# Edits at five places of an encoder layer on one core: first row, product order, bias table, rotation tables, a joint

## The chip, the core and the metric

One core of a Trainium2 chip runs the whole layer in one launch. The metric is the device time of the execution in microseconds; the median of three runs counts. TensorE (PE) multiplies, VectorE (DVE), ScalarE (ACT) and GpSimd (POOL) do the rest, and SyncE (SP), ACT and POOL issue DMAs.

## What is computed

A layer on x of 512 tokens by 1024 features, in float32: a feed-forward half step, a mixer of two attentions, a second feed-forward half step, and a last norm.

```python
def swiglu(x, w1, w3, w2):
    return (jax.nn.silu(x @ w1) * (x @ w3)) @ w2

x = x + 0.5 * swiglu(rmsnorm(x, ffn1_norm), w1, w3, w2)      # d_ff = 2816
x = x + hybrid_mixer(rmsnorm(x, mix_norm), ...)              # A and B below
x = x + 0.5 * swiglu(rmsnorm(x, ffn2_norm), w1, w3, w2)
return rmsnorm(x, final_norm)
# A: 3 groups x 8 heads, dilated windows; scores get bias_tab[t5_bucket(rel_steps * dilation)]
# B: 8 query heads on 2 key heads; q and k are RMS-normed, scaled by a gain, and rotated:
#    [x0 * cos - x1 * sin, x0 * sin + x1 * cos]
```

The bias of A depends only on the head and on the distance, so it is a table of 32 buckets by 24 heads, spread over 383, 255 and 255 distances for the three groups.

## The kernel before

**Numbers.** Every float32 product is made of three products of a shorter kind (fp32r). An operand X is split into a high part (a cast: wh, hH, TH) and a low part (X minus the high part: wl, hL, TL). `mm3` (L260) issues high by high, high by low and low by high: L262, L263 and L264 in every row. ACT does the casts (L247 for weights), DVE the low parts (L248).

**Layout and order.** x lies feature by token: eight rows x[d] of 128 features by 512 tokens. The order of PE is the order of the program (`manual_schedule`); the other engines' queues are ordered by the planner, by priority and by when it thinks an input ready. A tile is a buffer of a ring with a tag; a new tile in a full ring waits until all that read or wrote an earlier one has ended. Weights run through rings of three (wr raw, wh and wl split), loaded by SP and split some chunks ahead of PE.

**The start** (`layer`, from L1257). After four warm-up products (`idle`, L266), for each row d: SP loads x[d] and, for d < 4, the part of the first weights that multiplies it; `norm_h` (L406) makes hH on ACT, then hL on DVE (the norm's own factor comes in later, from the running squares); the weight part is cast on ACT (L1274) and its low part made on DVE (L1275). For d = 0 the weight part comes as two quarters of 256 columns, all on SP's queue behind x[0]. `quad` (L287) makes the first four features at once: for each row k, for each of four banks c, one mm3. It, and all features by `feat` (L277), use four main banks of PSUM (tag mm); four side banks (tag aux) serve the rest. What comes out of the first four features is held back until the norm's factor R is there (`stat_R`, a hook at step 33); feature 4 (f = 2) goes to a side bank meanwhile.

**The bias table.** After the first Strassen group, `blocks` multiplies by w2: eight output rows d, and at the end of row d = 0, 1 and 2 (`side`) `bias_rows(d)` is called (L683): SP loads the one-hot table and the mask into one tile of tag c1 (two buffers, shared with the Strassen accumulators); one PE product by `self.rel` (L692); DVE adds the mask in place (L693); POOL's queue stores the row from the tile to DRAM (L694). Rows 0 and 1 are interleaved (`sequence`, lag 2): row 0 ends, then two blocks of row 1, then row 1 ends. Later `bias_spread` copies the rows for the heads.

**The rotation tables** (`rope_tables`, L1043) are gain times cosine or sine, made on DVE in four token blocks, two halves, two functions and two gains, when PE is in the gate features; these are evicted by DVE as z (L730).

**The joint.** In `mixer`, w_out gives x its last addition row by row; `done_o(d)` (L1248) adds, makes hH and hL of the row, then, for d >= 4, `t_rows` (L867) combines rows d-4 and d into operands of the second feed-forward's Strassen steps (TH and TL, L884 and L885, and the upper half of hH, hL). PE goes on with steps A11, A12 (bank X, all rows of hH and hL), A11 of the next pair, S1 (bank Y, TH and TL).

Of the kernel before, what the change touches and what calls it, by code (L numbers as in the profile page):

```python
# [11 lines left out]
F32 = mybir.dt.float32  # L12
# [21 lines left out]
LAST = 2  # L34
WARM = 4
T = 512
# [34 lines left out]
class Layer:  # L71
    def __init__(self, ctx, tc, a):
# [20 lines left out]
        nc.vector.memset(self.eps, EPS)  # L93
        nc.scalar.activation(self.ones, self.ones, AF.Copy)
        self.r = c.tile([128, 8], F32, name="r")
# [191 lines left out]
    def quad(self, name, done):  # L287
        banks = [self.bank() for _ in range(4)]
        for k in range(NK):
            if k % 2 == 0:  # L290
                H, L = self.weights(name, k // 2)
            for c in range(4):
                s = slice(512 * (k % 2) + 128 * c, 512 * (k % 2) + 128 * c + 128)
                self.mm3(banks[c], H[:, s], L[:, s], self.hH[k], self.hL[k], k == 0, k == NK - 1)
                if k == NK - 1:
                    done[c](banks[c])
                yield

# [106 lines left out]

    def norm_h(self, d, g, n=T):  # L406
        nc = self.nc
        gc = self.par[:, g + d:g + d + 1]
        H, L, x = self.hH[d][:, :n], self.hL[d][:, :n], self.x[d][:, :n]
        self.lead = nc.scalar.activation(H, x, AF.Copy, scale=gc)  # L410
        nc.vector.scalar_tensor_tensor(L, x, gc, f32(H), op0=ALU.mult, op1=ALU.subtract)  # L411

# [69 lines left out]
    def ffn_run(self, s, gin, gnext, hooks, out=None, side={}):  # L482
# [193 lines left out]
    def bias_open(self, bp):  # L676
        self.bp = bp
        self.rel = bp.tile([32, 64], F32, name="rel_bias")[:, :24]
        self.nc.sync.dma_start(self.rel, self.a["rel_bias"])
        self.zd = self.dram.tile([8, 128, NV], F32, name="zd")  # L680
        self.vd = self.dram.tile([8, NV], F32, name="vd")

    def bias_rows(self, g):  # L683
        nc = self.nc
        n = (V0, V1, V2)[g]
        o = (0, V0, V0 + V1)[g]
        both = self.cp.tile([128, 1024], F32, tag="c1", name="bias")
        t = {"onehot": both[:32, :n], "vmask": both[:8, 512:512 + n]}
        for k in t:
            nc.sync.dma_start(t[k], self.a[k][:, o:o + n])  # L690
        ps = self.aux("bps")
        nc.tensor.matmul(ps[:8, :n], self.rel[:, 8 * g:8 * g + 8], t["onehot"], start=True, stop=True)  # L692
        nc.vector.scalar_tensor_tensor(t["vmask"], ps[:8, :n], 8.0, t["vmask"], op0=ALU.mult, op1=ALU.add)  # L693
        nc.gpsimd.dma_start(self.vd[:, o:o + n], t["vmask"])  # L694

# [171 lines left out]
    def t_rows(self, d):  # L867
# [14 lines left out]
        for src, H, L in ((raw[:, 0:3], self.TH[:, k], self.TL[:, k]),  # L882
                          (raw[:, 3], self.hH[k][:, 256:512], self.hL[k][:, 256:512])):
            nc.scalar.copy(H, src)  # L884
            nc.vector.tensor_sub(L, src, f32(H))  # L885

# [156 lines left out]
    def rope_tables(self, bp):  # L1043
# [6 lines left out]
        for w in range(2):  # L1050
            GC = bp.tile([128, 4, 2, 64], F32, name=f"GC{w}")
            GS = bp.tile([128, 4, 2, 64], F32, name=f"GS{w}")
            for i in range(4):
                for half in range(2):
                    for dst, e in ((GC, 0), (GS, 1)):
                        nc.vector.scalar_tensor_tensor(dst[:, i, half], gq[:, w, half], 1.0 if w else HD_B ** -0.5, cs[:, i, e],
                                                       op0=ALU.mult, op1=ALU.mult)
            self.tabs.append((GC, GS))
# [103 lines left out]
    def mixer(self):  # L1162
# [149 lines left out]
def constants():  # L1312
# [4 lines left out]
    ok = np.concatenate([np.abs(d0) <= 64, np.abs(d1) <= 64, d2 % 4 == 0])  # L1317
    onehot = (np.arange(N_BUCKETS)[:, None] == t5_bucket(rel)[None, :]).astype(np.float32)
    vmask = np.broadcast_to(np.where(ok, 0.0, 8.0 * NEG).astype(np.float32), (8, NV))
    t = np.arange(T)  # L1320
# [79 lines left out]
```

## Time and profile before

| | us |
|---|---|
| median of three runs | 1244.58 (1244.53 to 1245.4) |
| the profiled execution | 1244.16 |
| its span | 1242.4 |
| PE busy | 1233.9 |
| DVE busy | 906.8 |
| ACT busy | 605.8 |
| POOL busy | 126.5 |

The span runs from the first instruction to the last; the time has 1.8 us around it. Busy times overlap. A product's recorded duration reaches into the next one, so the pitch (start to start) tells what it costs PE; PEld is the weight load beside it. In a time line a bracket shows how long the engine was idle before a row and what ended that.

### The profile page before, as it was taken

The numbers are of one execution on the slowest core, as the hardware profiler recorded it, in microseconds if no ns is written. First come the engines' busy times: TensorE is split into PE (matmuls) and PEld (weight loads), VectorE is DVE, ScalarE is ACT, GpSimd is POOL, SyncE is SP. The second block draws the span as 40 slices with busy tenths as digits, with TensorE's granted clock in tenths as the row PEclk, the third lists the DMA queues.
The fourth block names the chain that finished last, engine by engine and source line by source line (L and its number), as shares of the span: only waits on it lengthen the run. The fifth ranks groups of instructions, "written<-read, shape, count | busy, mean of one in ns | idle before, by whom it ended". The sixth has DMA issues, their size and how long they took to land.

```text
span 1242.4 us, 20511 instructions
## 1 busy us (share of the span) xinstructions
PE 1233.9 (99%) x8228; PEld 1116.0 (90%) x8228; DVE 906.8 (73%) x1371; ACT 605.8 (49%) x897; POOL 126.5 (10%) x131
## 2 busy tenths in 40 slices
PE   9999999999999999999999999999999999999998
PEld 7897999899899999988888888888899989988997
DVE  6985688468787887567746888865988757875874
ACT  7652365245464444454424446664665425532554
POOL 1111101000222110200001200000211001100001
PEclk9999999999999999999999999999999999999999
DMA  8785777241388982662232231267768536744222
GB/s 292 220 217 166 194 195 194 92 119 52 136 222 251 231 229 97 223 183 79 87 116 100 68 119 43 71 218 241 208 170 203 157 99 188 189 149 111 60 85 68
DMA packets 90224, 190.85 MB, mean 154 GB/s; under 512 B 12801, under 2 KB 18577, under 8 KB 90129
## 3 DMA queue, kind: packets, MB, share of 16 engines
q1 hardware_dynamic: 70912, 145.46, 34.5%
q0 software_dynamic: 18496, 43.54, 17.6%
q8 instruction: 64, 1.05, 0.4%
q10 hardware_dynamic: 720, 0.55, 0.1%
q14 instruction: 32, 0.25, 0.1%
HBM read 175.79 MB, written 17.38 MB: 155 GB/s over the span
## 4 chain that ended last, share of the span: by engine, by line
PE 92%; DVE 3%; DMA 2%; issue 1%; ACT 0%; SPq 0%; POOL 0%; POOLq 0%; ACTq 0%; DVEq 0%
PE mm L262 23%; PE mm L264 22%; PE mm L263 22%; PE Y L263 4%; PE Y L262 4%; PE Y L264 4%; PE X L263 2%; PE X L264 2%; PE X L262 2%; DMA wt<-in_w13b 1%; PE S L925 1%; PE mm L1001 1%; PE Tb L1137 1%; PE T L1012 1%; DVE wl L248 1%
## 5 line engine op out<-in xcount | busy, mean ns | idle before, releaser
L247 ACT CAST wh<-wr 128x1024 fp32r<-128x1024 f32 x133 | 139.6, 1050 | 182.2 <-PE mm L263 124.1
L248 DVE TENSOR_TENSOR wl<-wr,wh 128x1024 fp32r<-128x1024 f32 x133 | 163.0, 1225 | 52.1 <-ACT wh L247 51.5
L262 PE MATMUL mm<-hH,wh 128*128 128x256 f32 (+1 forms) x560 | 179.7, 321 | 0.4 <-DVE t L509 0.3
L264 PE MATMUL mm<-hH,wl 128*128 128x256 f32 (+1 forms) x560 | 177.0, 316 | 0.0
L263 PE MATMUL mm<-hL,wh 128*128 128x256 f32 (+1 forms) x560 | 176.9, 316 | 0.0
L262 PE MATMUL mm<-gg,wh 128*128 128x512 f32 (+1 forms) x440 | 166.4, 378 | 0.0
L263 PE MATMUL mm<-gg,wh 128*128 128x512 f32 (+1 forms) x440 | 165.9, 377 | 0.0
L264 PE MATMUL mm<-gg,wl 128*128 128x512 f32 (+1 forms) x440 | 165.9, 377 | 0.0
L262 PEld LDWEIGHTS mm<-hH,wh 128*128 128x128 f32 x560 | 105.2, 188 | 9.9 <-ACT wh L1274 1.1
L264 PEld LDWEIGHTS mm<-hH,wl 128*128 128x128 f32 x560 | 105.2, 188 | 8.4 <-DVE wl L1275 0.4
L263 PEld LDWEIGHTS mm<-hL,wh 128*128 128x128 f32 x560 | 105.3, 188 | 7.4 <-DVE hL L411 0.2
L247 ACT CAST wh<-wa 128x1024 fp32r<-128x1024 f32 x54 | 56.8, 1051 | 96.3 <-PE mm L263 46.1
L262 PEld LDWEIGHTS mm<-gg,wh 128*128 128x128 f32 x440 | 82.6, 188 | 16.6 <-PE mm L264 0.9
L264 PEld LDWEIGHTS mm<-gg,wl 128*128 128x128 f32 x440 | 82.6, 188 | 15.3
L263 PEld LDWEIGHTS mm<-gg,wh 128*128 128x128 f32 x440 | 82.6, 188 | 15.0
L247 ACT CAST wh<-ws 128x1024 fp32r<-128x1024 f32 x54 | 56.8, 1052 | 71.3 <-PE mm L263 49.3
L247 ACT CAST wh<-wt 128x1024 fp32r<-128x1024 f32 x54 | 56.8, 1052 | 64.9 <-PE mm L263 41.4
L262 PE MATMUL mm<-TH,wh 128*128 128x256 f32 x320 | 88.4, 276 | 0.0
L263 PE MATMUL mm<-TL,wh 128*128 128x256 f32 x320 | 88.3, 276 | 0.0
L264 PE MATMUL mm<-TH,wl 128*128 128x256 f32 x320 | 88.3, 276 | 0.0
L248 DVE TENSOR_TENSOR wl<-wt,wh 128x1024 fp32r<-128x1024 f32 x54 | 65.9, 1222 | 28.7 <-ACT wh L247 27.9
L581 DVE TENSOR_TENSOR u<-mm,R 128x512 f32<-128x512 f32 x40 | 27.7, 691 | 75.7 <-PE mm L264 75.5
(280 smaller groups left out, 3240.6 us busy)
## 6 DMA issues: line engine op xcount, KB each, us to landing
wr<-in_w2a SPq DMA_DIRECT2D x22, 512.0 KB, 3.3
wt<-in_w13b SPq DMA_DIRECT2D x22, 512.0 KB, 3.5
wa<-in_w13b SPq DMA_DIRECT2D x22, 512.0 KB, 3.3
wt<-in_w13b POOLq DMA_DIRECT2D x22, 512.0 KB, 6.0
wr<-in_w2b SPq DMA_DIRECT2D x22, 512.0 KB, 3.7
wt<-in_w13a SPq DMA_DIRECT2D x18, 512.0 KB, 3.8
wt<-in_w13a POOLq DMA_DIRECT2D x18, 512.0 KB, 7.1
wa<-in_w13a SPq DMA_DIRECT2D x18, 512.0 KB, 3.9
```

Of the source, the lines that this page charges most:

```text
L247: self.nc.scalar.copy(H, raw)
L248: self.nc.vector.tensor_sub(L, raw, f32(H))
L262: mm(out, lH, rH, start=start, stop=False, skip_group_check=more)
L263: mm(out, lH, rL, start=False, stop=False, skip_group_check=more)
L264: mm(out, lL, rH, start=False, stop=stop, skip_group_check=more)
L581: nc.vector.tensor_mul(u, ps, R)
L925: nc.tensor.matmul(*args, start=True, stop=True)
L1001: nc.tensor.matmul(oc, v, p, start=st, stop=sp)
L1012: nc.tensor.transpose(ps[:, 128 * b:128 * b + 128], P[h][:, c0 + 128 * b:c0 + 128 * b + 128], self.ident)
L1137: nc.tensor.transpose(pt[:, 128 * j:128 * j + 128], P[h, j][:, 128 * k:128 * k + 128], self.ident)
```

## The change

At the start, x row 0's weight quarters are loaded from ACT's queue, ahead of the row loop, and the dummy activation on `ones` moves behind them; a warm-up product goes. `norm_h` for row 0 makes only hH, one half of the columns on ACT and one on DVE; DVE casts the first weight quarter; then comes hL (`low`), and low parts of weights are queued behind hL. `quad` issues, for all rows but the last, first the four high by high products, then the four with hL, then the four with wl. Feature 5 goes to a side bank as feature 4 does. The bias table becomes an fp32r product over 64 rows: the table's high part over its low part, and the one-hot table twice, cast on ACT into a tile of its own (counts made even by zero columns). The rotation tables are made for four token blocks in one operation. At the joint, one low part of TL (k = 2, made in `t_rows(6)`) is put off until behind row 7's hL.

```diff
-WARM = 4
+WARM = 3
-        nc.scalar.activation(self.ones, self.ones, AF.Copy)      # in __init__
 quad:
+            terms = [(w, h, c) for w, h in ((H, self.hH[k]), (H, self.hL[k]), (L, self.hH[k])) for c in range(4)]
+            for n, (w, h, c) in enumerate(terms):
+                self.nc.tensor.matmul(banks[c], w[:, s[c]], h, start=k == 0 and n < 4, stop=False)
+                if n % 3 == 2:
+                    yield
 norm_h:
+        if first:
+            nc.scalar.activation(H[:, :256], x[:, :256], AF.Copy, scale=gc)
+            nc.vector.tensor_scalar(H[:, 256:], x[:, 256:], gc, None, op0=ALU.mult)
+            return
 plain:
-                yield from self.feat("w13" + s, 2 * f + 1, later(done3))
+                yield from self.feat("w13" + s, 2 * f + 1, later(done3), f == 2)
 bias_open:
+        raw = bp.tile([64, 32], F32, name="rel_bias")[:, :24]
+        self.rel = bp.tile([64, 32], F32R, name="relr")[:, :24]
+        for e in range(2):
+            nc.sync.dma_start(raw[32 * e:32 * e + 32], self.a["rel_bias"])
+        with self.tc.issue_after(self.lead.ins):
+            nc.scalar.copy(self.rel, raw)
+        with self.tc.issue_after(self.lowest.ins):
+            nc.vector.tensor_sub(self.rel[32:64], raw[32:64], f32(self.rel)[32:64])
 bias_rows:
         both = self.cp.tile([128, 1024], F32, tag="c1", name="bias")
-        t = {"onehot": both[:32, :n], "vmask": both[:8, 512:512 + n]}
+        m, vmask = (n + 1) // 2 * 2, both[:8, 512:512 + n]
+        nc.sync.dma_start(both[:64, :m], self.a["onehot"][:, o + g:o + g + m])
+        nc.sync.dma_start(vmask, self.a["vmask"][:, o:o + n])
+        onehot = self.cp.tile([128, 1024], F32R, tag="c1", name="onehot")[:64, :m]
+        nc.scalar.copy(onehot, both[:64, :m])
-        nc.tensor.matmul(ps[:8, :n], self.rel[:, 8 * g:8 * g + 8], t["onehot"], start=True, stop=True)
+        nc.tensor.matmul(ps[:8, :m], self.rel[:, 8 * g:8 * g + 8], onehot, start=True, stop=True)
 t_rows:
+            if k == 2 and src.shape[1] == 3:
+                self.owed = (L, src, f32(H))
 rope_tables:
-            for i in range(4):
-                for half in range(2):
+            for half in range(2):
+                g = gq[:, w, half].unsqueeze(1).to_broadcast([128, 4, 64])
+                for dst, e in ((GC, 0), (GS, 1)):
+                    nc.vector.scalar_tensor_tensor(dst[:, :, half], g, 1.0 if w else HD_B ** -0.5, cs[:, :, e],
+                                                   op0=ALU.mult, op1=ALU.mult)
 done_o:
+            if d == 7:
+                with tc.issue_after(self.lowest.ins):
+                    nc.vector.tensor_sub(*self.owed)
 layer:
+        for s in (slice(0, 256), slice(256, 512)):
+            nc.scalar.dma_start(self.raws[0][:, s], self.a["w13a"][0][:, s])
+        nc.scalar.activation(self.ones, self.ones, AF.Copy)
-            for s in parts:
+            for s in parts[:len(parts) * d]:
                 nc.sync.dma_start(self.raws[d // 2][:, s], self.a["w13a"][d // 2][:, s])
-            self.norm_h(d, G_FFN1)
+            self.norm_h(d, G_FFN1, first=d == 0)
-                nc.scalar.copy(H[:, s], raw[:, s])
-                nc.vector.tensor_sub(L[:, s], raw[:, s], f32(H)[:, s])
+                (nc.scalar.copy if d or s.start else nc.vector.tensor_copy)(H[:, s], raw[:, s])
+                if d == 0 and s.start == 0:
+                    self.low(d, G_FFN1, T)
+                with tc.issue_after(self.lowest.ins):
+                    nc.vector.tensor_sub(L[:, s], raw[:, s], f32(H)[:, s])
```

## Rows read from the trace of the kernel before

**Rows 1.** The page, busy times and instructions of each engine.
```profile
PE 1233.9 (99%) x8228; PEld 1116.0 (90%) x8228; DVE 906.8 (73%) x1371; ACT 605.8 (49%) x897; POOL 126.5 (10%) x131
```

**Rows 2.** Time line, start: start, us, engine, line, operation, out<-in, count [idle before <-releaser].
```profile
1.32 3.78 PE L269 MATMUL warm<-R 128*128 128x256 f32 x8 [1.32 <-POOL R L97]
3.90 0.72 ACT L410 ACTIVATE hH<-x,par 128x512 fp32r<-128x512 f32 x1 [1.22 <-DMA par<-in_par]
4.96 0.80 PE L262 MATMUL mm<-hH,wh 128*128 128x512 f32 x1
5.28 0.40 ACT L1274 CAST wh<-wr 128x256 fp32r<-128x256 f32 x1 [0.36 <-DMA wr<-in_w13a]
5.56 0.61 PE L263 MATMUL mm<-hL,wh 128*128 128x512 f32 x1
6.01 0.40 PE L264 MATMUL mm<-hH,wl 128*128 128x512 f32 x1
6.24 0.40 PE L262 MATMUL mm<-hH,wh 128*128 128x512 f32 x1
6.60 0.72 ACT L410 ACTIVATE hH<-x,par 128x512 fp32r<-128x512 f32 x1 [0.92 <-DMA x<-in_x]
...
11.69 0.39 PE L262 MATMUL mm<-hH,wh 128*128 128x512 f32 x1
```

**Rows 3.** Time line, a DVE operation of 256 columns.
```profile
905.15 0.42 DVE L877 SCALAR_TENSOR_TENSOR Traw<-Traw 128x256 f32<-128x256 f32 x1
```

**Rows 4.** Windows: stretch; busy PE, PEld, DVE, ACT, POOL; clock, DMA share, GB/s.
```profile
2.00:4.00 2.00, 2.00 (x6) 1.59 (x5) 0.00 (x0) 0.77 (x3) 0.00 (x0) 1.00 0.85 245
4.00:5.00 1.00, 1.00 (x4) 0.38 (x2) 0.35 (x1) 0.91 (x2) 0.00 (x0) 1.00 0.67 156
```

**Rows 5.** Time line, PE at 35 us.
```profile
34.59 0.39 PE L264 MATMUL mm<-hH,wl 128*128 128x512 f32 x1
35.25 0.50 PE L262 MATMUL mm<-hH,wh 128*128 128x512 f32 x1 [0.27 <-DVE t L509]
```

**Rows 6.** The chain that ended last: start, us, what; the bias products.
```profile
99.62 0.73 PE bps L692 x2
...
101.94 0.52 PE bps L692 x2
...
108.15 0.52 PE bps L692 x2
```

**Rows 7.** Waits of SP's queue, 82 to 112 us: total, times, longest.
```profile
SPq L690 <- DMA vd<-bias: 5.0, 1, 5.0
```

**Rows 8.** Time line, the first store and the third load of the bias table.
```profile
101.23 0.58 POOL L694 DMA_DIRECT2D vd<-bias  x1 [17.58 <-DVE bias L693]
...
103.06 0.31 SPq L690 DMA_DIRECT2D bias<-in_onehot  x1
```

**Rows 9.** Line L1056's cosine operations (as many sine ones); time line, PE behind them.
```profile
L1056 DVE SCALAR_TENSOR_TENSOR GC<-gq,cs x16: 217/218/226, 638.9 to 643.0; 128x64 f32<-128x64 f32 x16
...
643.31 0.39 PE L264 MATMUL mm<-wh,hL 128*128 128x512 f32 x1
644.00 0.50 PE L262 MATMUL mm<-wh,hH 128*128 128x512 f32 x1 [0.30 <-DVE z L730]
```

**Rows 10.** Time line, the joint.
```profile
902.68 0.95 DVE L885 TENSOR_TENSOR TL<-Traw,TH 128x768 fp32r<-128x768 f32 x1
...
903.55 0.74 DVE L411 SCALAR_TENSOR_TENSOR hL<-x,par,hH 128x512 fp32r<-128x512 f32 x1
...
904.35 0.38 PE L263 MATMUL X<-hL,wh 128*128 128x256 f32 x1 [0.26 <-DVE hL L411]
...
909.03 0.95 DVE L885 TENSOR_TENSOR TL<-Traw,TH 128x768 fp32r<-128x768 f32 x1
```

**Rows 11.** Windows, the joint, columns as above.
```profile
904.30:907.90 3.60, 3.55 (x31) 3.56 (x32) 3.60 (x8) 3.02 (x5) 1.10 (x1) 1.00 0.34 120
```

**Rows 12.** Windows, the end of the span.
```profile
1238.00:1239.00 1.00, 0.00 (x0) 0.00 (x0) 0.26 (x1) 0.00 (x0) 0.26 (x1) 0.57 0.94 307
```

More of the change, by code (lines that the diff above doesn't have):

```diff
@@ L291, in quad @@
                 H, L = self.weights(name, k // 2)
[L292 to L295, printed above, removed]
-                    done[c](banks[c])
-                yield
+            last = k == NK - 1
+            s = [slice(512 * (k % 2) + 128 * c, 512 * (k % 2) + 128 * c + 128) for c in range(4)]
+            if last:
+                for c in range(4):
+                    self.mm3(banks[c], H[:, s[c]], L[:, s[c]], self.hH[k], self.hL[k], False, True)
+                    done[c](banks[c])
+                    yield
+                continue
+            terms = [(w, h, c) for w, h in ((H, self.hH[k]), (H, self.hL[k]), (L, self.hH[k])) for c in range(4)]
+            for n, (w, h, c) in enumerate(terms):
+                self.nc.tensor.matmul(banks[c], w[:, s[c]], h, start=k == 0 and n < 4, stop=False)
+                if n % 3 == 2:
+                    yield
     def token(self, name, n, toks, done):
@@ L404, in weave, with norm_h, low @@
                 next(fill, None)
-    def norm_h(self, d, g, n=T):
+    def norm_h(self, d, g, n=T, first=False):
         nc = self.nc
         gc = self.par[:, g + d:g + d + 1]
+        H, x = self.hH[d][:, :n], self.x[d][:, :n]
+        if first:
+            nc.scalar.activation(H[:, :256], x[:, :256], AF.Copy, scale=gc)
+            nc.vector.tensor_scalar(H[:, 256:], x[:, 256:], gc, None, op0=ALU.mult)
+            return
+        self.lead = nc.scalar.activation(H, x, AF.Copy, scale=gc)
+        self.low(d, g, n)
+    def low(self, d, g, n):
         H, L, x = self.hH[d][:, :n], self.hL[d][:, :n], self.x[d][:, :n]
-        self.lead = nc.scalar.activation(H, x, AF.Copy, scale=gc)
-        nc.vector.scalar_tensor_tensor(L, x, gc, f32(H), op0=ALU.mult, op1=ALU.subtract)
+        self.lowest = self.nc.vector.scalar_tensor_tensor(L, x, self.par[:, g + d:g + d + 1], f32(H), op0=ALU.mult, op1=ALU.subtract)
     def norm_sq(self, d, pool=NK - 2):
@@ L677, in bias_open @@
         self.bp = bp
-        self.rel = bp.tile([32, 64], F32, name="rel_bias")[:, :24]
-        self.nc.sync.dma_start(self.rel, self.a["rel_bias"])
+        nc = self.nc
+        raw = bp.tile([64, 32], F32, name="rel_bias")[:, :24]
[6 more added lines that the diff above has]
+            nc.vector.tensor_sub(self.rel[32:64], raw[32:64], f32(self.rel)[32:64])
         self.zd = self.dram.tile([8, 128, NV], F32, name="zd")
@@ L687, in bias_rows @@
         both = self.cp.tile([128, 1024], F32, tag="c1", name="bias")
-        t = {"onehot": both[:32, :n], "vmask": both[:8, 512:512 + n]}
-        for k in t:
-            nc.sync.dma_start(t[k], self.a[k][:, o:o + n])
+        m, vmask = (n + 1) // 2 * 2, both[:8, 512:512 + n]
[3 more added lines that the diff above has]
+        nc.scalar.copy(onehot, both[:64, :m])
         ps = self.aux("bps")
-        nc.tensor.matmul(ps[:8, :n], self.rel[:, 8 * g:8 * g + 8], t["onehot"], start=True, stop=True)
-        nc.vector.scalar_tensor_tensor(t["vmask"], ps[:8, :n], 8.0, t["vmask"], op0=ALU.mult, op1=ALU.add)
-        nc.gpsimd.dma_start(self.vd[:, o:o + n], t["vmask"])
+        nc.tensor.matmul(ps[:8, :m], self.rel[:, 8 * g:8 * g + 8], onehot, start=True, stop=True)
+        nc.vector.scalar_tensor_tensor(vmask, ps[:8, :n], 8.0, vmask, op0=ALU.mult, op1=ALU.add)
+        nc.gpsimd.dma_start(self.vd[:, o:o + n], vmask)
     def bias_spread(self, h):
@@ L884, in t_rows @@
             nc.scalar.copy(H, src)
-            nc.vector.tensor_sub(L, src, f32(H))
+            if k == 2 and src.shape[1] == 3:
+                self.owed = (L, src, f32(H))
+            else:
+                nc.vector.tensor_sub(L, src, f32(H))
     def until(self, fill, item):
@@ L1052, in rope_tables @@
             GS = bp.tile([128, 4, 2, 64], F32, name=f"GS{w}")
-            for i in range(4):
-                for half in range(2):
-                    for dst, e in ((GC, 0), (GS, 1)):
-                        nc.vector.scalar_tensor_tensor(dst[:, i, half], gq[:, w, half], 1.0 if w else HD_B ** -0.5, cs[:, i, e],
-                                                       op0=ALU.mult, op1=ALU.mult)
+            for half in range(2):
[3 more added lines that the diff above has]
+                                                   op0=ALU.mult, op1=ALU.mult)
             self.tabs.append((GC, GS))
@@ L1318, in constants @@
     onehot = (np.arange(N_BUCKETS)[:, None] == t5_bucket(rel)[None, :]).astype(np.float32)
+    onehot = np.insert(onehot, (V0, V0 + V1, NV), 0.0, axis=1)
+    onehot = np.concatenate([onehot, onehot])
     vmask = np.broadcast_to(np.where(ok, 0.0, 8.0 * NEG).astype(np.float32), (8, NV))
```

## The prediction

> **What bounds the kernel now.** I read the page's busy times first, then the chain that ended last, then the time line wherever TensorE (PE) has a hole, and the wait lists of the queues that feed it. PE is busy 1233.9 of 1242.4 us, DVE 73%, ACT 49% [rows 1], and the chain runs through PE nearly everywhere. So a part of this change pays only if it removes PE work or closes a hole in PE's stream. The unit is the pitch of a 512-column product: 0.23 us from start to start (6.01 to 6.24 [rows 2]). The holes that the change aims at are in five places: the first 12 us, 35 us, three bias products at 99 to 109 us, 643 us and 904 us. None is over 1.3 us, so the whole change can be worth 3 to 4 us of 1244, no more; the danger is a new hole.
>
> **1. The first row.** Today the first product starts at 4.96; the 24 products of input rows 0 and 1 end when row 2 starts at 11.69. That is 6.73 us for 24 x 0.23 = 5.5, so 1.2 us is all there is: slow first products, and waits for the parts of row 1 [rows 2]. The change (a) splits the scaling of row 0 over ScalarE (ACT) and VectorE (DVE); (b) casts the first weight quarter on DVE; (c) issues both weight quarters of row 0 on ACT's queue, so that the next rows' loads move up by two issues on SP; (d) orders the products by kind, so that low parts are wanted four or eight products later; (e) drops one of four warm-up products (ending near 4.2 instead of 5.1). The table load on ACT now stands behind the two issues; ACT's first real work waits for the input at 3.90 anyway, which hides it. For (a) and (b) I count two DVE operations of 256 columns at 0.42 [rows 3] from 3.90: a first product near 4.7, 0.26 earlier. (d) takes away most of the waits for low parts. Against it stands (c). The second weight quarter landed at 5.28 [rows 2] while it was ahead of x row 1 on one queue; on another queue it shares the DMA engines with x row 1. In the engines' share there is room for (1-0.85) x 2 + (1-0.67) x 1 = 0.63 us between 2 and 5 us [rows 4], which earlier issues can fill; so the quarter lands between 5.3 and 6.6, when x row 1 landed [rows 2], and columns 3 and 4 of the first row wait for it. If it lands at 6.6, its cast (0.40 [rows 2]) ends at 7.0 and 22 products remain: 7.0 + 22 x 0.23 = 12.0, a loss of 0.3. If all goes well, 1.1 is gained. I take **-0.4** (between -1.1 and +0.6), since the quarter is more likely delayed by half a row than by none or by a whole one.
>
> The Trainium skill, "Trainium Kernel Development and Optimization", Key Constraints, says that DMAs issued from several engines' queues run on the same 16 DMA engines and interleave, so that a second queue saves issue time alone. By that rule no byte moves faster, and only the 0.63 us above can come back. The trace agrees so far as the share is below 1 before 5 us. The sum would be the same with -0.6 as the most that (c) can bring.
>
> **2. A side bank for the sixth feature product.** At 35.25 PE waits for DVE to free one of the four main banks: 34.59 to 35.25 is 0.66, which is 0.43 more than the pitch, and the first product behind a wait takes 0.50 instead of 0.39, another 0.11 [rows 5]. With a bank of the other pool there is nothing to wait for; the next product that needs a main bank starts 24 x 0.23 = 5.5 us later, when DVE has emptied several. **-0.54** (-0.54 to -0.2, if some other user of the four side banks comes late).
>
> **3. The bias table.** PE spends 0.73, 0.52 and 0.52 us on the three bias products, each a float32 product in two recorded passes [rows 6]. As one pass of 384, 256 and 256 columns they should take their share of the pitch, 0.17, 0.12 and 0.12, plus some 0.03 each: an estimate of **-1.3**. The additions are a cast of the one-hot table on ACT (0.4 us each, beside work with slack) and, this is the point, **a second tile per call from the same two-buffer tag c1**. Before, a call took one such tile; successive calls alternated. Now call 0 takes both buffers: its raw table and mask in one, the cast table in the other. Call 1 needs two again, and the first is held until call 0's result has been stored, because the stored row lies in that tile. That a new tile waits for this store is in the trace: SP's bias load stood 5.0 us behind the DMA vd<-bias [rows 7]. It was call 2's, and cost nothing, for PE came to that product only at 108.15. But calls 0 and 1 are only 101.94 - 99.62 = 2.32 us apart on PE [rows 6], because the first two output rows end with their last two blocks side by side. So: the store of call 0 is issued at 101.23 by GpSimd's queue and its landing frees SP at 103.06 [rows 8]. Neither moves up by a faster product: the DVE operation ahead of it waits behind another eviction. From 103.06 the cast of call 1 (0.40) gives a product at 103.5. PE would be there at 101.94 - 0.53 = 101.4. **New wait: +2.1 us.** That holds if call 1's raw table went into the buffer that call 0's cast table freed at about 99.9 and landed meanwhile. If it must go into the buffer that the store frees, its load starts only at 103.06 and needs a landing more; the store's own, 101.23 to 103.06, is 1.8, and I take 2.0: **+4.1**. Behind PE's wait in program order stand all following products. Behind SP's waiting load stand weight loads, which stood 5.0 us there before and held nobody up [rows 7]; behind ACT's waiting cast stand casts that fill three buffers (wh) ahead of PE; behind DVE's waiting bias operation one eviction, of a bank that PE wants again four rows later. I cost these at nothing; without that cover PE's wait would grow by a weight split of 1024 columns, at most 4 x 0.42 = 1.7 us [rows 3]. Call 2 comes 108.15 - 101.94 = 6.2 us after call 1, against a chain of about the same length in the late case and a shorter one in the other: 0 to 0.3. Lower end: nothing at all, if the tile can be had earlier than I read. Net of product and wait **+0.8** (-1.3 to +3.1).
>
> **4. Rotation tables.** 32 operations of 64 columns hold DVE from 638.9 to past 643 and with it the eviction for which PE waits at 644.00: 643.31 to 644.00 is 0.69, less 0.23, plus 0.11: 0.57 [rows 9]. Eight operations of 256 columns at no more than 0.42 [rows 3] take at most 3.4 us instead of 4.3; that is 0.9 less, more than the wait. **-0.57** (-0.57 to -0.4).
>
> **5. The low part at the joint.** At 904.35 PE waits for the low part of row 7, which DVE starts at 903.55, behind a low part of 0.95 us started at 902.68 that is not wanted until five microseconds later [rows 10]. Swapped, row 7 is ready near 903.4, and PE's 0.5 us goes. But DVE has no idle time there (3.60 of 3.60 us between 904.3 and 907.9 [rows 11]): the same operations in another order end at the same time, and the last of them that PE wants, the low part begun at 909.03 and done at 909.98 [rows 10], is late already: PE stands for it. PE arrives there 0.5 us sooner and waits 0.5 us longer. **0** (0 to -0.76 if the planner now happens to put that last low part ahead of the weight split before it; to +0.3 if the shift puts something else last).
>
> **The sum.** -0.4 - 0.54 + 0.8 - 0.57 + 0 = -0.71. The profiled execution took 1244.16 us (span 1242.4); it would take 1243.45. The median of the runs is 0.42 above it, so I forecast **1243.9 us**; its own spread is 1242.7 to 1245.0.
>
> **The rivals.** (A) *The bias calls don't wait*: then the sum is -2.8, **1241.8**. For it: the raw and the cast table could come out of the buffers in an order that I don't see. Against it: the 5.0 us of SP behind the store [rows 7]. (B) *The load itself waits for the store*: two microseconds more, **1245.9**. For it: a ring taken strictly in turn would do that, and before, calls took turns. Against it: the other buffer is free 3 us sooner. (C) *PE's clock falls in that wait.* The first products, after the warm-up from 1.32, stand 0.45 apart at 5.56 and 0.23 apart from 6.01 [rows 2]: half clock (1.2 GHz) for about 4.6 us, and then 2.4 GHz. (The windows show a granted clock of 1.00 before 5 us [rows 4]; I go by the pitch.) At the end of the span the granted clock is 0.57 in the slice from 1238 to 1239, in which PE has no product any more [rows 12]. If a wait at 101 us did the same, 4.6 us at half clock would lose 2.3 us: with B **1248.2**, slower than before. In the tail PE has stood without products for about two microseconds by then, and the short wait of 2.1 barely reaches that; so I give the fall to the long one. The Trainium skill, "TensorE: Matmul & The Clock Gate", Part 1, says that "the default state is throttled, and activity releases the throttle"; the trace agrees at both ends and has no case in the middle.
>
> **How the numbers follow.** Forecast 54%, A 15%, B 19%, C 12%. A change under 0.2% (2.5 us) is about what a measurement of this kernel can't tell from none: below 1242.1 counts as faster, above 1247.1 as slower. Faster: most of A, and a little of the forecast's tail where the start and the joint both bring their best: 0.15. Slower: C and a little of B: 0.13. Same: 0.72. The range takes in A and B and leaves C out: 1241.3 to 1247.0.
>
> **What would show it.** On PE: a wait before the second bias product near 101 us, with ACT's cast of onehot as releaser and that cast behind the DMA vd<-bias; three bias products under 0.25 us. No wait at 35 and 644 us. At the joint, none at X and a longer one at Y. Early: row 2 starting at 11.3, with the third column of row 0 waiting for a cast. I am wrong if the second bias product follows the first within 2 us, if PE's pitch behind it is 0.45, or if row 2 starts after 11.7.

## The result and the profile after

The changed kernel takes 1247.94 us (median of eight runs, 1247.06 to 1249.77) against 1244.81 for the kernel before beside it: ratio 1.0027, 95% interval 1.0019 to 1.0036. It is slower by 3.1 us, where 0.7 us less was forecast. The profiled execution took 1248.29 us, 4.13 more than that of before. The first fence is the page's busy times, to be held against [rows 1]: PE has five products fewer and is busy 1.2 us longer. The second is the span and the mean granted clock.

```profile
PE 1235.1 (99%) x8223; PEld 1118.5 (90%) x8223; DVE 905.6 (73%) x1350; ACT 606.0 (49%) x900; POOL 125.5 (10%) x131
```
```profile
core 0: 1246.5 us, clock 0.997
```

Since PE's order of work is the same in both kernels, apart from the order inside the first feature group, I lined up the products of the two traces, name by name, and read at each how much later it starts in the kernel after. That difference moves at few places:

| place | start before -> after | how much later |
|---|---|---|
| first product | 4.96 -> 5.72 | 0.75 |
| statistics product, start of the stage behind | 25.29 -> 27.23 | 1.94 |
| after the sixth feature | 54.53 -> 55.90 | 1.37 |
| behind bias product 0 | 100.28 -> 101.18 | 0.90 |
| bias product 1 | 101.87 -> 104.84 | 2.97 |
| behind it | 102.39 -> 105.05 | 2.66 |
| bias product 2 | 108.08 -> 112.30 | 4.22 |
| behind it | 108.60 -> 112.51 | 3.91 |
| third group's scores, before and after | 376.11 -> 379.84, 596.73 -> 601.85 | 3.73, 5.11 |
| behind the rotation tables | 665.24 -> 669.73 | 4.49 |
| behind X at the joint | 906.06 -> 910.01 | 3.95 |
| behind Y | 911.72 -> 915.92 | 4.20 |

**The start.** The time line of the kernel after, for [rows 2]:

```profile
1.32 2.93 PE L268 MATMUL warm<-R 128*128 128x256 f32 x6 [1.32 <-POOL R L96]
3.75 0.35 DVE L418 TENSOR_SCALAR hH<-x,par 128x256 fp32r<-128x256 f32 x1 [2.82 <-DMA par<-in_par]
5.28 0.29 DVE L1306 CAST wh<-wr 128x256 fp32r<-128x256 f32 x1 [1.18 <-DMA wr<-in_w13a]
5.72 1.19 PE L301 MATMUL mm<-hH,wh 128*128 128x512 f32 x2 [1.47 <-DVE wh L1306]
6.63 0.40 ACT L1306 CAST wh<-wr 128x256 fp32r<-128x256 f32 x1 [2.38 <-DMA wr<-in_w13a]
7.09 1.22 PE L301 MATMUL mm<-hH,wh 128*128 128x512 f32 x2 [0.19 <-ACT wh L1306]
8.11 1.91 PE L301 MATMUL mm<-hL,wh 128*128 128x512 f32 x4
9.82 1.23 PE L301 MATMUL mm<-hH,wl 128*128 128x512 f32 x4
```

The scaling of x row 0 starts at 3.75, but the first weight quarter comes at 5.27 (before, ACT cast it at 4.52) and the second at 6.63 (before 5.28). PE has no product from 4.25, the end of the warm-up, to 5.72. And the four products from 8.11 to 9.82 take 1.71 us, 0.43 each: half clock (1.2 GHz), until 10.2; before, the pitch is 0.23 from 6.01. Row 2 begins at 13.63 instead of 11.69. That this is half clock I read from the pitch: the windows of this trace give a granted clock of 1.00 here too, as they do before 5 us in [rows 4]. In the second trace of the same kernel, described below, the same pitch stands at a granted clock of 0.50. First the window of this trace, then that of the second (columns as in [rows 4]; the clock stands third from the end):

```profile
7.10:10.10 3.00, 3.00 (x7) 2.42 (x8) 2.80 (x5) 3.00 (x6) 0.00 (x0) 1.00 1.01 397
```
```profile
8.10:11.40 3.30, 3.30 (x9) 2.58 (x8) 3.10 (x6) 3.15 (x7) 0.00 (x0) 0.50 1.03 405
```

**The bias table.** PE's waits from 100 to 110 us (total, times, longest), ACT's from 100 to 109, those of SP's queue from 100 to 106, and the time line:

```profile
PE bps L715 <- ACT onehot L713: 2.0, 1, 2.0
```
```profile
ACT onehot L713 <- DMA vd<-bias: 0.7, 1, 0.7
```
```profile
SPq L710 <- PE bps L715: 1.9, 1, 1.9
```
```profile
100.91 0.34 PE L715 MATMUL bps<-onehot,relr 64*8 64x384 f32 x1
101.28 0.47 SPq L710 DMA_DIRECT2D bias<-in_onehot  x1
102.47 0.58 POOL L717 DMA_DIRECT2D vd<-bias  x1 [17.38 <-DVE bias L716]
104.38 0.40 ACT L713 CAST onehot<-bias 64x256 fp32r<-64x256 f32 x1 [0.69 <-DMA vd<-bias]
104.84 0.28 PE L715 MATMUL bps<-onehot,relr 64*8 64x256 f32 x1 [2.00 <-ACT onehot L713]
105.05 0.50 PE L261 MATMUL mm<-gg,wh 128*128 128x512 f32 x1
...
105.97 0.63 PE L261 MATMUL mm<-gg,wh 128*128 128x512 f32 x1
106.40 0.63 PE L262 MATMUL mm<-gg,wh 128*128 128x512 f32 x1
```

The raw table of call 1 is loaded at 101.28: SP's queue waits 1.9 us for the product of call 0, which reads call 0's cast table, and not for the store. The cast of call 1 into the second tile waits until the store of call 0 has landed, and starts 1.92 us after that store's issue. PE stands between the product at 102.45 and the one at 104.84. From 105.97 the pitch is 0.43. The windows:

```profile
104.00:105.60 1.60, 0.76 (x3) 0.57 (x4) 1.60 (x3) 0.40 (x1) 0.00 (x0) 1.00 0.00 0
105.60:109.00 3.40, 3.40 (x10) 2.61 (x9) 0.27 (x1) 0.00 (x0) 0.53 (x1) 0.51 0.59 186
109.00:111.00 2.00, 2.00 (x10) 1.68 (x9) 0.00 (x0) 0.41 (x1) 0.00 (x0) 0.98 0.00 0
```

**The other places.** At 35 us the pitch stays 0.23. At 644 us PE waits no more: DVE makes the tables in eight operations of 0.42. At the joint the wait of [rows 10] is gone, and one at Y has come, in which PE wants another low part (L911, not the one that was put off):

```profile
644.00 0.43 DVE L1082 SCALAR_TENSOR_TENSOR GC<-gq,cs 128x256 f32<-128x256 f32 x1 [2.90 <-DMA gq<-in_gqk]
913.75 0.28 PE L261 MATMUL Y<-TH,wh 128*128 128x256 f32 x1
914.23 0.38 PE L262 MATMUL Y<-TL,wh 128*128 128x256 f32 x1 [0.20 <-DVE TL L911]
```

### The profile page after: what moved, and what is told of

Read it like the earlier page. It is cut to its first block, busy times and chain, and to the rows that moved or that the text cites. A ratio compares the mean times of both kernels' runs of the same rounds, so it can differ in the third digit from the quotient of the medians.

```text
span 1246.5 us, 20485 instructions
## 1 busy us (share of the span) xinstructions
PE 1235.1 (99%) x8223; PEld 1118.5 (90%) x8223; DVE 905.6 (73%) x1350; ACT 606.0 (49%) x900; POOL 125.5 (10%) x131
## 4 chain that ended last, share of the span: by engine, by line
PE 98%; issue 1%; DMA 1%; DVE 0%; POOL 0%; ACTq 0%; ACT 0%; POOLq 0%; DVEq 0%
PE mm L261 24%; PE mm L263 24%; PE mm L262 24%; PE Y L262 4%; PE Y L263 4%; PE Y L261 4%; PE X L263 2%; PE X L262 2%; PE X L261 2%; PE mm L301 2%; PE S L951 1%; PE mm L1027 1%; PE Tb L1163 1%; PE T L1038 1%; PE Sb L263 1%
## 5 line engine op out<-in xcount | busy, mean ns | idle before, releaser
L261 PE MATMUL mm<-hH,wh 128*128 128x256 f32 (+1 forms) x532 | 168.2, 316 | 0.0
L263 PE MATMUL mm<-hH,wl 128*128 128x256 f32 (+1 forms) x532 | 166.0, 312 | 0.0
L262 PE MATMUL mm<-hL,wh 128*128 128x256 f32 (+1 forms) x532 | 165.9, 312 | 0.0
L261 PEld LDWEIGHTS mm<-hH,wh 128*128 128x128 f32 x532 | 99.9, 188 | 7.2 <-issue 0.9
L263 PEld LDWEIGHTS mm<-hH,wl 128*128 128x128 f32 x532 | 99.9, 188 | 6.8
L262 PEld LDWEIGHTS mm<-hL,wh 128*128 128x128 f32 x532 | 100.0, 188 | 6.1
```

Source lines behind the costliest of these rows:

```text
L261: mm(out, lH, rH, start=start, stop=False, skip_group_check=more)
L262: mm(out, lH, rL, start=False, stop=False, skip_group_check=more)
L263: mm(out, lL, rH, start=False, stop=stop, skip_group_check=more)
```

## The experiments

Three questions: what the wait and the clock at 105 us hang on, what makes the start late, and whether the 1.4 us at the scores come from the change. Each ratio is taken against the kernel before, run beside it on the same chip; those medians of before lay between 1244.2 and 1246.1 us, so across experiments only ratios are compared.

**The mask and the result in a tile of their own** (on the changed kernel):

```diff
-        m, vmask = (n + 1) // 2 * 2, both[:8, 512:512 + n]
+        m, vmask = (n + 1) // 2 * 2, self.tmp.tile([128, T], F32, tag="t", name="vmask")[:8, :n]
```

> The changed kernel with one edit: the bias mask, and with it the result that is stored, gets a tile of its own, so that the raw table's c1 buffer is free as soon as ACT has cast it. Theory (the second bias product waits for the store of the first because they share a c1 buffer): ACT's cast of call 1 no longer waits for the DMA vd<-bias, the second bias product starts near 102.5 instead of 104.84, and with no hole there the granted clock does not fall to half behind it; gain 2.07 (wait) + 1.56 (half clock) = 3.6 us, some 1244.3. Rival (the wait comes from GpSimd's store queue or from the load of the next raw table itself): the product still starts at 104.8 and the time stays near 1247.9. Second rival (the clock falls around 105 us whatever PE does): gain 2.1 only, 1245.8.

Ratio 0.9997 (0.9985 to 1.0009), from 1.0027: 0.30% (about plus or minus 0.15), 3.7 us. Time line and windows:

```profile
100.83 0.34 PE L715 MATMUL bps<-onehot,relr 64*8 64x384 f32 x1
101.21 0.41 ACT L713 CAST onehot<-bias 64x256 fp32r<-64x256 f32 x1 [3.52 <-PE bps L715]
102.69 0.28 PE L715 MATMUL bps<-onehot,relr 64*8 64x256 f32 x1
```
```profile
105.60:109.00 3.40, 3.40 (x16) 2.49 (x15) 0.86 (x3) 0.56 (x1) 0.53 (x1) 1.00 0.57 163
```

The cast no longer waits for the store, the product stands at PE's own pace, the clock stays at 1.00. Wait and fall both came from the shared tile. The start in this trace is late as in the kernel after (1.86 at the statistics product).

**The bias part alone, on the kernel before** (`bias_open`, `bias_rows` and the host's one-hot table as in the diff ahead of the prediction, its core being):

```diff
-        t = {"onehot": both[:32, :n], "vmask": both[:8, 512:512 + n]}
+        m, vmask = (n + 1) // 2 * 2, both[:8, 512:512 + n]
+        onehot = self.cp.tile([128, 1024], F32R, tag="c1", name="onehot")[:64, :m]
+        nc.scalar.copy(onehot, both[:64, :m])
```

> The kernel before with the bias part of the change alone (table split in high and low parts, one product per call, the cast table in a second c1 tile, the result still in the first). Theory (the wait and the fall of the clock belong to this part): wait of about 2.1 us at the second product behind the store, products 1.1 us shorter, so 1.0 us slower than before where the clock holds and 2.5 us slower where it falls to half for 3.4 us; ratio 1.001 to 1.002, and the rest of the trace as before, the scores of the third attention pass among it. Rival (the wait needs the later start or the other parts): ratio 0.999.

Ratio 1.0022 (1.0013 to 1.0031): this part alone makes the kernel slower by 2.7 us. In its trace products 0 and 1 stand 3.94 apart (99.46 and 103.40), the cast starts 1.93 after the store's issue, and the pitch is 0.43 from 104.14 to 107.1. It needs neither the later start nor the other parts. At the scores, which the expectation had as before, this trace loses 1.84 us; the second traces below bear on that.

**Filler products ahead of the second bias product** (on the changed kernel), seen in two traces:

```diff
+        if g == 1:
+            self.idle(4, 256)
         ps = self.aux("bps")
```

> The changed kernel with one edit: four products of the warm-up's kind (256 columns of float32, results not used) stand on PE directly before the second bias product, so that PE has work in the first 1.7 us of its wait; the wait for ACT's cast stays. Theory (the clock falls because PE has no product for 2.4 us): the second bias product still starts at 104.8, the granted clock stays at 1.00 behind it, the pitch behind it is 0.23 instead of 0.43, gain about 1.5 us, some 1246.4. Rival (the fall hangs on something else than the hole, as on the store or the loads): half clock from 105.7 to 109.1 as before, time near 1247.9.

> The run with filler products ahead of the second bias product once more. In the first trace the store of call 0 took 3.3 us to land instead of 1.8, which hid what the filler did. Theory (the store's time varies from execution to execution): it lands after about 1.8 here, the hole behind the filler is near 0.4 us, the clock holds, and PE comes out of it 1.5 us earlier than the changed kernel. Rival (the filler itself delays the store or the cast): 3.3 again.

Ratio 1.0024 (1.0012 to 1.0036), no gain that can be told. The clock held in both traces, with 2.15 and 1.48 from the last filler's start to the bias product's. But the cast began 3.41 and 2.74 us after the store's issue, where the five traces with the wait and without filler have 1.89 to 1.93; the store itself landed after 3.3 and 2.6 us instead of 1.8. So the second expectation, that it would land after 1.8, fell, and PE's wait, longer by 1.5 and 0.8 us, took back most of the 1.56 that the clock gained in the first trace, and half of it in the second. Why the store lands later beside the filler stays open.

**The weight quarters back on SP's queue** (on the changed kernel):

```diff
-        for s in (slice(0, 256), slice(256, 512)):
-            nc.scalar.dma_start(self.raws[0][:, s], self.a["w13a"][0][:, s])
-            for s in parts[:len(parts) * d]:
+            for s in parts:
```

> The changed kernel with one edit: the two weight quarters of input row 0 are issued by SP again, between x row 0 and x row 1, as before the change; the split scaling, the order by kind and three warm-up products stay. Theory T1 (the second queue makes the quarters late): they land by 4.5 and 5.3 instead of 5.27 and 6.63, the first product starts near 4.7 instead of 5.72, the third feature's hole of 0.8 goes, gain 1.0 to 2.0 us, 1246 to 1247. Theory T2 (one warm-up product less leaves PE without work before 5.7, and half clock then lasts until 10.1): the first product may come sooner, but the pitch stays 0.43 until about 10, gain under 0.7 us.

Ratio 1.0001 (0.9991 to 1.0011). The first quarter is cast at 4.01, the second at 5.33, the first product starts at 4.45; but the pitch is 0.43 until 10.2, and the statistics product is still 1.34 late. The trace goes with theory T2; the ratio, 0.26% lower (about plus or minus 0.13, or 3.2 us plus or minus 1.6), with T1, and more. Part of that is the clock behind the bias wait. In this trace the hole there is as long as in the kernel after (2.36 against 2.39), and the clock did not fall:

```profile
105.60:109.00 3.40, 3.40 (x17) 2.81 (x16) 0.00 (x0) 0.00 (x0) 0.50 (x1) 1.00 0.52 173
```

The mean granted clock of each execution on record says more than one trace can. A stretch of 3.4 us at half clock takes 1.7 us, or 0.0014 of the span, off that mean (an estimate from the windows above). It is 0.997 in five of this kernel's ten executions, 0.998 in one and 0.999 in four; with the mask apart it is 0.998 or 0.999 in all ten, in the kernel after 0.996 to 0.998 in all eight. So such a stretch seems to come in some executions of one kernel and not in others. The 0.6 us at the start and half of the 1.56 make 1.4 of the 3.2 us; the rest is not explained.

**Four warm-up products** (on the changed kernel):

```diff
-WARM = 3
+WARM = 4
```

> The changed kernel with one edit: four warm-up products as before the change, instead of three. Theory T2 (the missing warm-up product): PE works until about 5.1, the granted clock rises near 6 to 7 us instead of 10.1, gain 1.0 to 1.5 us, some 1246.7, with the first product still at 5.7 since its weight quarter still lands at 5.27. Theory T1 (late quarters alone, the clock rises late because of the holes that they make): clock and first product stay as in the changed kernel, time near 1247.9.

Ratio 1.0023 (1.0013 to 1.0033). First product at 6.04 (5.72 in the kernel after), pitch 0.43 until 10.2, row 2 at 13.63, the last two as in the kernel after: theory T2, the missing warm-up product, fell for this edit by itself.

**Both, with the mask apart** (the three edits above together).

> The changed kernel with three edits together: the bias mask and result in a tile of their own (as in the run with the mask apart), row 0's weight quarters back on SP's queue between x rows 0 and 1, and four warm-up products. Neither of the last two moved the start by itself by more than 0.6 us: with early quarters PE still stood without work before the first product, with four warm-up products the quarters still came late; in both the pitch stayed 0.43 until about 10 us. Theory (PE must be busy without a hole from the warm-up on, and it takes both for that): first product near 4.5, 0.23 pitch from about 6, the start ends 0 to 0.5 us before that of the kernel before, so about 3 us less than before in all (0.7 from the other parts as the run with the mask apart showed them, and 1.9 from its start): ratio 0.9975 to 0.998. Rival (the order by kind and the split scaling make the holes that hold the clock down, by the third product's wait for the second quarter): pitch 0.43 until about 10, start 1.3 us late, ratio 0.999.

Ratio 0.9983 (0.9974 to 0.9992), faster than before. PE's time line at the start:

```profile
3.61 1.49 PE L268 MATMUL warm<-R 128*128 128x256 f32 x3
4.56 1.47 PE L301 MATMUL mm<-hH,wh 128*128 128x512 f32 x4
5.87 1.09 PE L301 MATMUL mm<-hL,wh 128*128 128x512 f32 x4
6.80 1.09 PE L301 MATMUL mm<-hH,wl 128*128 128x512 f32 x4
9.08 0.73 PE L301 MATMUL mm<-hH,wh 128*128 128x512 f32 x2 [1.19 <-ACT wh L1304]
```

No hole behind the warm-up, and full pitch from 5.17. But row 0 done early is no gain: PE then stands 1.19 us, until the weights of row 1 are cast, and row 2 begins at 11.94.

**The old start, with the mask apart**, and the same with the products by kind (on the changed kernel; the first also has `quad` as before):

```diff
-WARM = 3
+WARM = 4
-        for s in (slice(0, 256), slice(256, 512)):
-            nc.scalar.dma_start(self.raws[0][:, s], self.a["w13a"][0][:, s])
-            for s in parts[:len(parts) * d]:
+            for s in parts:
-            self.norm_h(d, G_FFN1, first=d == 0)
+            self.norm_h(d, G_FFN1)
-                (nc.scalar.copy if d or s.start else nc.vector.tensor_copy)(H[:, s], raw[:, s])
...
+                nc.scalar.copy(H[:, s], raw[:, s])
...
-        m, vmask = (n + 1) // 2 * 2, both[:8, 512:512 + n]
+        m, vmask = (n + 1) // 2 * 2, self.tmp.tile([128, T], F32, tag="t", name="vmask")[:8, :n]
```

> The changed kernel with its whole first part undone (scaling of row 0, first cast, queue of the quarters, order of the products and four warm-up products as in the kernel before) and the bias mask in a tile of its own. Theory: the start is that of the kernel before to 0.1 us, no wait at the bias products, and what is left is the side bank (-0.57), the bias products (-1.1), the tables (-0.6) and the joint (-0.3), in all -2.6 us: ratio 0.998. Rival (some of these gains are eaten further on, as at the scores of the third attention pass, where the changed kernel lost 1.4 us more): ratio 0.999 or above.

> As the run with the whole first part undone, but with the products still in the order by kind, so that this order alone stands against it. Theory (low parts wanted later): the 0.26 and 0.16 us that PE waits for low parts in the kernel before go, but the third product now wants the second weight quarter at once, so the start gains or loses no more than 0.5 us. Rival (the third product's wait for the second quarter keeps the clock at half): pitch 0.43 until about 10 us, a start some 1.3 us later than with the old order.

Ratios 0.9984 (0.9975 to 0.9992) and 0.9981 (0.9972 to 0.9990); row 2 at 11.22 and 11.57. All three kernels without the wait and with four warm-up products behind early quarters beat the kernel before by some 2 us; they can't be told apart, so order by kind and split scaling neither gain nor lose anything that these runs could show. Against the run with the mask apart, which differs from the first of the two by the start alone, the new start costs 0.13% (1.6 us); with about plus or minus 0.15% on it the times alone don't show that cost. The two traces do: 2.3 us at the statistics product.

**Single edits of the start, on the kernel before.** The queue alone (the diff); three warm-up products alone (`WARM = 3`); both; the queue with the order by kind (`quad` as in the change):

```diff
-        nc.scalar.activation(self.ones, self.ones, AF.Copy)
...
+        for s in (slice(0, 256), slice(256, 512)):
+            nc.scalar.dma_start(self.raws[0][:, s], self.a["w13a"][0][:, s])
+        nc.scalar.activation(self.ones, self.ones, AF.Copy)
         self.idle(WARM, 256)
-            for s in parts:
+            for s in parts[:len(parts) * d]:
```

> The kernel before with one edit of the first part alone: the two weight quarters of row 0 are issued by ACT, ahead of its table load, instead of by SP between x rows 0 and 1 (scaling, casts, order and four warm-up products as before). Theory (the second queue is what makes the quarters late, since the later rows' loads are issued earlier and share the DMA engines with them): the first quarter lands at 5.3 to 6.2 instead of 4.5, the second at 6.6 to 7.7 instead of 5.3, the first product starts 0.8 to 1.7 us later, and PE, idle since 5.1, stays at half clock until about 9.5 to 10; row 2 begins 1.5 to 2.5 us later and the kernel is that much slower: ratio 1.001 to 1.002. Rival (the quarters are late only together with the split scaling or the order by kind): row 2 begins as before, ratio 1.000.

> The kernel before with three warm-up products instead of four and nothing else. Theory W (PE's clock stays at half when the warm-up ends at 4.25 and the first product follows near 4.9): the pitch stays 0.43 until about 10 us, row 2 begins near 13 instead of 11.7, ratio 1.001. Theory Q (it takes the late quarters as well, since the hole here is only 0.7 us): full pitch from about 6, row 2 at 11.6 to 11.9, ratio 1.000.

> The kernel before with row 0's two weight quarters on ACT's queue and three warm-up products. Theory W and theory Q alike: first product at 5.8 to 6.6 after a hole of 1.5 to 2.4 us behind the warm-up, pitch 0.43 until about 10, row 2 near 13.6, 1.5 to 2 us late, ratio 1.0012 to 1.0016. Theory K (the order by kind is needed for it, since it makes the third product wait for the second quarter): no more than 0.5 us late at row 2, ratio 1.000.

> The kernel before with row 0's two weight quarters on ACT's queue and the products in the order by kind; four warm-up products. Theory K: the third product waits for the second quarter (a hole of 0.5 to 1.5 us behind the second product), the pitch is 0.43 until about 10, row 2 near 13.6, ratio 1.0012 to 1.0016. Theory W: four warm-up products hold the clock, the hole is made up before row 1 is there, row 2 at 11.9 to 12.2, ratio 1.000.

| kernel | first product | pitch 0.23 from | row 2 | ratio |
|---|---|---|---|---|
| before | 4.96 | 6.01 | 11.69 | |
| queue | 6.25 | 6.59 | 11.86 | 1.0002 (0.9993 to 1.0011) |
| three warm-up products | 4.79 | 9.14 | 12.34 | 1.0000 (0.9991 to 1.0010) |
| queue, three products | 5.64 | 5.98 | 11.69 | 1.0006 (0.9997 to 1.0015) |
| queue, by kind | 5.52 | 7.79 | 12.57 | 1.0007 (0.9998 to 1.0016) |
| after | 5.72 | 10.18 | 13.63 | 1.0027 (1.0019 to 1.0036) |

PE with late quarters and nothing else changed (waits from 2 to 12 us, total, times, longest):

```profile
PE mm L261 <- ACT wh L1276: 1.2, 1, 1.2
```

The quarters are late by the queue alone (cast at 5.79 and 7.00), as the theory of that run said, but it costs 0.17 us at row 2, not 1.5 to 2.5: at full clock the 24 products of rows 0 and 1 follow each other without a hole, and the wait only takes the place of later ones. With three warm-up products alone the trace has theory W's pitch until 8.9, but the time doesn't show its price; with both, the half clock that W and Q expect didn't come; by kind, theory K's hole came (1.60 from start to start) and its half clock didn't. In the traces no single edit and no pair has row 2 as late as the whole; the times can't rank them, for the intervals reach up to 1.0016. Row 2 at 12.34 and at 13.63 goes with half clock through row 0, and whether that comes varies between executions as well. With four warm-up products the pitch is 0.23 by 6.6 us in seven of nine traces; in the eighth (queue, by kind) it is from 7.79, behind the hole at the third product; in the ninth (four products on the changed kernel) from 10.2. With three, five of eight traces have 0.43 until 9 to 12 us, two begin with 0.31 and have 0.43 behind a hole at the third product, and one has 0.23 from 5.98.

**Both kernels once more**, for a second trace.

> The kernel before once more, for a second trace of it. Theory (the 0.2 to 1.4 us that every other trace loses at the scores of the third attention pass, between 560 and 603 us, is a row of DMA round trips that come out longer in some executions, and the first trace of before had it short): this trace shows some of it too, 0.5 to 1.5 us against the first trace of the same kernel. Rival (the changes cause it): nothing there, within 0.1 us.

> The changed kernel once more, for a second trace of it. Theory: first quarter lands after 5.2 again, the second product of the bias table waits about 2.1 us again behind the store. Whether the clock falls there is open: with holes of 2.36 to 2.40 us it fell in three traces and held in one, so it may do either; what it costs is 1.5 to 1.6 us where it falls and nothing where it holds.

In its second trace the kernel before starts the products behind the two scores stages 1.03 and 1.83 us later than in its first, counted from 0.21 at the statistics product. So the 1.38 us there need no cause in the change. PE's time line, scores of the first of the two stages in the second trace (in the first trace these 32 products begin at 566.89 and take 2.13 us):

```profile
567.10 3.16 PE L925 MATMUL S<-qk 64*128 64x128 f32 x32
```

The second trace differs in one more place. At X, where the first trace of before has the wait of [rows 10], PE goes on 0.12 us behind the product before it:

```profile
905.73 0.28 PE L262 MATMUL X<-hH,wh 128*128 128x256 f32 x1
905.85 0.38 PE L263 MATMUL X<-hL,wh 128*128 128x256 f32 x1
```

So 0.4 us are gained at X there without any edit, and as much in the traces of all five kernels that differ from the kernel before at the start or the bias table alone. The same comparison bears on the side bank: with the queue edit alone, and in both pairs with it, the wait at 35 us is gone (0.57 us at the sixth feature), though feature 5 has no side bank there.

In its second trace the changed kernel had its first product at 6.04 (5.72 in the first), the first two products 0.31 apart, and a pitch of 0.43 from 8.15 to 11.1, behind a hole at the third. At the bias table the cast starts 1.92 behind the store, products 0 and 1 stand 3.92 apart, and half clock follows (pitch 0.43 from 107.2 to 110.2).

## Why the prediction was wrong

Of the three signs that the text had set for being wrong, two came: the pitch behind the second bias product is 0.43, and row 2 starts after 11.7.

**1. The first row: the step that failed first.** Forecast -0.4, at worst +0.6; measured +1.94. The arrival was right: the quarter landed at 6.63, where the working had 6.6 for the bad case, its cast ended at 7.0, and the third product followed at 7.09. Then came "22 products remain: 7.0 + 22 x 0.23 = 12.0", and row 2 began at 13.63. The pitch was wrong: from 7.09 to 13.63 are 6.54 us for 22 products, where 22 x 0.23 is 5.06; the 1.5 us between them lie in the first seven, 0.36 to 0.59 apart. The text named a warm-up that ends near 4.2 instead of 5.1 and gave it no price; half clock was priced for 101 us and not for the place where the rows showed it. That the shorter warm-up is the cause is not shown: with four products in the changed kernel the trace has half clock just as long. The first quarter's lateness (5.27 for 4.52) was missed too. In both kernels it is issued at 1.2; it lands 2.9 us later in the one before, 4.1 us later in the one after; row 1's weights are issued at 1.65 instead of 2.59. The working gave the 0.63 us of free share to the quarters; that the loads moved up on SP took it is argued from these times, not measured by itself. The rule cited there, that transfers of several queues interleave on the same DMA engines (the Trainium skill, "Trainium Kernel Development and Optimization", Key Constraints), speaks for just this, and the traces agree: with the queue alone the first quarter is cast 1.3 us later.

**2. The side bank.** -0.54 forecast, -0.57 measured. With the old start the side bank does this without the queue edit (0.58 in the run with the old start and the mask apart); on the kernel before, the queue edit alone does it as well (0.57), which the forecast did not see.

**3. The bias table.** The wait: 2.1 forecast, 2.07 measured, with the releaser, the shared tile and the freed buffer as argued, so rivals A (no wait) and B (load behind the store) fall. The products: -1.3 forecast, -0.47 - 0.31 - 0.31 = -1.09 measured; from their start to the next product they take 0.27, 0.21 and 0.21 us, not 0.20, 0.15 and 0.15. The clock: **the second step that failed**. Rival C had the mechanism, and the text set it aside with "I give the fall to the long one". The short wait did it, in four of the five traces that have it, for 1.56 us instead of the 2.3 priced. With the wait this makes the part +2.5 instead of +0.8; alone it measured +2.7. C's time, 1248.2, is near the measured one by another sum: its long wait did not come.

**4. The rotation tables.** -0.57 forecast, -0.62 measured; against the second trace of before it would be -0.48.

**5. The joint.** 0 forecast, -0.54 at X and +0.25 at Y measured, so -0.29: inside the bounds. But 0.4 of the gain at X is not the edit's, since every other trace with the old joint has it. Against those the edit gains 0.13 at X and loses 0.25 at Y: about 0.1 us lost, near the 0 of the forecast, and Y waits for more than X gave up.

**The sum.** 1.94 - 0.57 - 1.09 + 2.07 + 1.56 - 0.62 - 0.29 = 3.0, against 3.1 between the medians. The profiled execution of after has 1.38 more at the scores and 0.2 less elsewhere: the 4.2 at Y. All these terms are held against one trace of the kernel before, so the closeness of 3.0 and 3.1 is in part luck. Three terms were right to 0.05 us (side bank, wait, tables), the products' and the joint's to 0.3; two, both half clock for the most part, turned 0.7 less into 3.1 more.

**What stays open**: which combination of the start's edits brings the half clock. The traces go best with the number of warm-up products: pitch 0.43 beyond 7 us in seven of eight traces with three, in one of nine with four. But the one with four has the whole rest of the change, and three alone take no more time than before (1.0000, 0.9991 to 1.0010). Open is also by what the clock decides in a hole of 2.4 us, since one trace held it.

## What to carry to other kernels

A tile that is both read early and stored late holds its ring buffer for the longer of the two; before a second tile of the same tag is added, ask what the first one still carries, and give the late part a tile of its own. Price a new hole of PE like the one here, 2.4 us from start to start, with half clock behind it (1.56 us in four of five traces), and ask at the start of a kernel, too, at which pitch the first products will run. And have a second trace of the kernel before: here it showed that 1.4 us at the scores and 0.4 us at the joint, both seen between the first two traces, come without the change as well.

## What was not expected of the hardware

Behind a hole of 2.36 to 2.40 us between products, PE ran at half clock for 3.4 us in four traces and kept full clock in one. A store of 12 KB on POOL's queue landed 1.8 us after its issue in the five traces with the wait, and 3.3 and 2.6 us after it in the two in which filler products ran on PE. Two executions of one kernel differed by 1.8 us at the scores of one attention pass. On ACT's queue the weight quarter that was wanted first landed 4.1 us after its issue in the kernel after, against 2.9 on SP's queue before.
